# A last block whose attention heads go through the array in pairs, in a fixed order among the projections

## The chip, the cores and the metric

The kernel runs on one core of a Trainium2 chip. The metric is the device time of one execution in microseconds (us). A core has five engines that run their own queues in order and wait for each other by semaphores: TensorE (PE in the profile; its weight loads are listed apart as PEld) multiplies matrices, VectorE (DVE) and ScalarE (ACT) work elementwise and empty PSUM, the memory that TensorE writes, GpSimd (POOL) works elementwise out of SBUF, and SyncE (SP) starts DMA transfers.

## The reference

256 tokens of 1024 channels in float32 go through three blocks: a first layer of two parallel mixers, a layer of latent attention, each followed by a squared-ReLU feed-forward part, and then the last block, which the change touches:

```
def chunk_relpos_attention(h, w_qkv, w_o, rel_bias):   # 16 heads of 64
    q, k, v = split_heads(h, w_qkv)
    ...
    for c in range(n_chunks):                          # chunks of 64 queries
        sc = einsum('bhqd,bhkd->bhqk', q_blk, k[:, :, k0:k1]) / sqrt(64)
        p = softmax(sc + bias, axis=-1)                # bias by relative position, per head
        outs.append(einsum('bhqk,bhkd->bhqd', p, v[:, :, k0:k1]))
    return merge_heads(o) @ w_o

x = x + rms_norm(chunk_relpos_attention(rms_norm(x, g), w_qkv, w_o, rel_bias), g_post)
x = x + rms_norm((silu(h @ w_gate) * (h @ w_up)) @ w_down, g_post_ffn)
```

With 256 tokens a query chunk sees all keys up to its own chunk. Every product is float32.

## The kernel before

Activations lie in SBUF with 128 channels on the partitions: `xh` and `xl` hold x as a high and a low part, and each weight block is split in the same way as it streams in, `whi` on ScalarE (line 149) and `wlo` on VectorE or GpSimd (line 152, class `Stream`). A product is then three fast matmuls, high by high, high by low, low by high. `mgemm` (lines 419 to 451) computes 256 tokens by 512 outputs, with the tokens as weights of the array and 512 weight columns streaming: eight blocks of 128 input channels (k), two token tiles, three matmuls each, into two PSUM banks. `tgemm_tok` (lines 453 to 491) does this for 1024 outputs in four banks; its first four k go in 8 steps (k by token tile) of two column halves, its last four k tile by tile. PSUM is used through two rings of four banks, `mmt()` and `auxt()`.

The stage in question is the value projection (two calls of `mgemm`, 512 outputs each), the attention of 16 heads, and the output projection (`tgemm_tok`). A head needs four steps: `sc` (scores of 256 queries in two tiles: the first against 128 keys, the second against 256; heads alternate between the upper and lower 64 partitions of `qT` and `kT`; VectorE adds the bias and takes the maximum, ScalarE takes exponentials and sums), `nrm` (VectorE scales by the reciprocal sum), `tr` (three 128x128 transposes on TensorE, copied out by VectorE for even and ScalarE for odd heads) and `pv` (probabilities times values, 64 output rows; after an odd head ScalarE and VectorE split the pair into `yh` and `yl`). These products are plain float32 matmuls, not split ones, and the profile shows each as two records. `attend(i)` issues `tr(i-3)`, `pv(i-4)`, `nrm(i-1)`, `sc(i)`. Three such calls are handed to `later`, a list of callbacks that run after so many microseconds of issued matmuls, in the second value projection; the rest follow after it, and four are issued within the output projection. In what order an engine's queue holds this work is decided by a scheduler, by a simulated time line; only the output projection's TensorE queue is kept in the order of the code (`manual_schedule`, before `tgemm_tok`).

Of the kernel before, what the change touches and what calls it, by code (L numbers as in the profile page):

```python
# [10 lines left out]
F32 = mybir.dt.float32  # L11
F32R = mybir.dt.float32r
# [6 lines left out]
P = 128  # L19
# [174 lines left out]
def block_kernel(ctx, tc, a, out):  # L194
# [18 lines left out]
    def mmt():  # L213
        return mm.tile([P, 512], F32, tag="mm", name="mm")

    def auxt():
        return aux.tile([P, 512], F32, tag="aux", name="aux")
# [198 lines left out]
        if b:  # L416
            S.done()

    def mgemm(h, l, nk, evac, per=4, psum=None, apart=False):


        pss = [(psum or mmt)() for _ in range(2)]
        n = nk // per

        def part(tt, k, w):
            wh, wl = w
            s = slice(k % per * 512, (k % per + 1) * 512)
            ts = slice(tt * P, (tt + 1) * P)
            pe.matmul(pss[tt], h[k][:, ts], wh[:, s], start=k == 0, stop=False)  # L429
            pe.matmul(pss[tt], h[k][:, ts], wl[:, s], start=False, stop=False)  # L430
            pe.matmul(pss[tt], l[k][:, ts], wh[:, s], start=False, stop=k == nk - 1)  # L431
            later.tick(0.65)

        if apart:
            ws = [S.get() for _ in range(n)]
            S.done(held=n)
            for tt in range(2):
                for k in range(nk):
                    part(tt, k, ws[k // per])
                evac(tt, pss[tt])  # L440
        else:
            for c in range(n):
                w = S.get()
                for k in range(c * per, (c + 1) * per):
                    for tt in range(2):
                        part(tt, k, w)
                if c < n - 1:
                    S.done()
            for tt in range(2):
                evac(tt, pss[tt])  # L450
        S.done()

    def tgemm_tok(h, l, nk, evac, psum, pre={}):
# [12 lines left out]

        step = 0
        for k in range(nk - 4):
            if k % 2 == 0:
                w = S.get()  # L470
            for tt in range(2):
                if step in pre:
                    pre[step]()
# [418 lines left out]
    with tc.tile_pool(name="mla", bufs=1) as ap:  # L892
# [229 lines left out]
    ss = b2.tile([P, 2, 2], F32, name="ss")  # L1122
    ss2 = b2.tile([P, 2, 2], F32, name="ss2")
    r1 = b2.tile([P, 2], F32, name="r1")

    def row(i):

# [12 lines left out]
    with tc.tile_pool(name="cra", bufs=1) as ap, tc.tile_pool(name="crt", bufs=2) as mp:  # L1140
# [15 lines left out]
        qT = ap.tile([P, 8, T], F32, name="qT")  # L1156
        kT = ap.tile([P, 8, T], F32, name="kT")
        v = ap.tile([P, 2, D], F32, tag="v", name="v")
        yh = ap.tile([P, KB, T], F32R, name="yh")
        yl = ap.tile([P, KB, T], F32R, name="yl")  # L1160
        R = ap.tile([P, 2], F32, name="R")

        def qk_chain():
# [26 lines left out]
        def qk_out(m, ps):  # L1190
            g = ps.shape[1]
            for i in range(g):
                j = m + i
                dst, rb = (qT[:, j], rbc[1]) if j < 8 else (kT[:, j - 8], rbc[0])
                state["qk"] = dve.tensor_tensor(dst, ps[:, i], rb, op=ALU.mult)

        later(3.5, qk_chain)
# [6 lines left out]
        st_p, st_t = {}, {}  # L1204

        QS = (slice(0, P), slice(P, 3 * P))

        def sc(h):
            ps = mmt()
            rr = slice(64 * (h % 2), 64 * (h % 2) + 64)  # L1210
            j = h // 2
            pe.matmul(ps[:, QS[0]], qT[rr, j, 0:P], kT[rr, j, 0:P], start=True, stop=True)
            pe.matmul(ps[:, QS[1]], qT[rr, j, P:T], kT[rr, j], start=True, stop=True)
            mx = mp.tile([P, 2], F32, tag="mx", name="mx", bufs=3)
            nm = mp.tile([P, 2], F32, tag="nm", name="nm", bufs=3)
            sm = mp.tile([P, 2], F32, tag="sm", name="sm", bufs=4)
            sb = mp.tile([P, 3 * P], F32, tag="sb", name="sb", bufs=2)
            pr = mp.tile([P, 3 * P], F32, tag="pr", name="pr", bufs=4)
            dve.tensor_tensor_reduce(sb[:, QS[0]], ps[:, QS[0]], B[:, h, P:T], op0=ALU.add, op1=ALU.max,
                                     scale=1.0, scalar=-3.0e38, accum_out=mx[:, 0:1])  # L1220
            dve.tensor_tensor_reduce(sb[:, QS[1]], ps[:, QS[1]], B[:, h], op0=ALU.add, op1=ALU.max,
                                     scale=1.0, scalar=-3.0e38, accum_out=mx[:, 1:2])
            dve.tensor_scalar(nm, mx, -1.0, None, op0=ALU.mult)
            for qt in range(2):
                act.activation(pr[:, QS[qt]], sb[:, QS[qt]], AF.Exp, bias=nm[:, qt:qt + 1],
                               accum_out=sm[:, qt:qt + 1])
            st_p[h] = (pr, sm)

        def nrm(h):
            pr, sm = st_p[h]  # L1230
            dve.reciprocal(sm, sm)
            for qt in range(2):
                dve.tensor_scalar(pr[:, QS[qt]], pr[:, QS[qt]], sm[:, qt:qt + 1], None, op0=ALU.mult)

        def tr(h):
            pr, sm = st_p.pop(h)
            ps = auxt()
            for i in range(3):
                pe.transpose(ps[:, i * P:(i + 1) * P], pr[:, i * P:(i + 1) * P], ident)
            pT = mp.tile([P, 3 * P], F32, tag="pT", name="pT", bufs=2)  # L1240
            (act.activation(pT, ps[:, 0:3 * P], AF.Copy) if h % 2 else dve.tensor_copy(pT, ps[:, 0:3 * P]))
            st_t[h] = pT

        def pv(h):
            pT = st_t.pop(h)
            if h % 2 == 0:
                state["o"] = auxt()
            o = state["o"]
            rr = slice(64 * (h % 2), 64 * (h % 2) + 64)
            hc = slice(h * 64, (h + 1) * 64)  # L1250
            pe.matmul(o[rr, 0:T], v[:, 0, hc], pT[:, 0:T], start=True, stop=False)  # L1251
            pe.matmul(o[rr, P:T], v[:, 1, hc], pT[:, T:3 * P], start=False, stop=True)
            if h % 2:
                j = h // 2
                S.behind = act.activation(yh[:, j], o[:, 0:T], AF.Copy)
                dve.tensor_tensor(yl[:, j], o[:, 0:T], yh[:, j].bitcast(F32), op=ALU.subtract)

        def attend(i):
            if 0 <= i - 3 < NH:
                tr(i - 3)  # L1260
            if 0 <= i - 4 < NH:
                pv(i - 4)
            if 0 <= i - 1 < NH:
                nrm(i - 1)
            if i < NH:
                sc(i)
# [4 lines left out]
        mgemm(XH, XL, KB, v_evac(0))  # L1271
        for i in range(3):
            later(3.8 + 2.0 * i, lambda i=i: attend(i))
        mgemm(XH, XL, KB, v_evac(1), psum=auxt)
        later.flush()
        for i in range(3, NH):
            attend(i)

        mix_row = row(1)

# [17 lines left out]
        def x_feat(tt, b):  # L1298
# [16 lines left out]
        mctx = tc.manual_schedule(engines={mybir.EngineType.PE})  # L1315
        mctx.__enter__()
        tgemm_tok(per_k(yh), per_k(yl), KB, wo_evac, mmt,
                  pre={2: lambda: attend(16),4: lambda: attend(17),6: lambda: attend(18),7: lambda: attend(19)})


    with tc.tile_pool(name="swi", bufs=1) as ap, tc.tile_pool(name="swt", bufs=2) as mp:
# [181 lines left out]
```

## Time and profile before

| | us |
|---|---|
| median of 3 runs | 928.31 (924.77, 928.31, 928.44) |
| profiled execution | 924.32 |
| its span, first to last instruction | 922.6 |
| TensorE busy | 898.3 |
| VectorE, ScalarE, GpSimd busy | 588.8, 482.8, 253.8 |
| mean granted TensorE clock | 0.994 of full speed |

Times within the span are us from its start. The profile's records of matmuls overlap, since they are pipelined; how fast TensorE goes is read from the distance between starts, not from the length of a record.

### The profile page before, as it was taken

The page shows a single profiled execution, that of the slowest core. Times are in us where ns is not written, and L with a number is a line of the kernel's source. Part 1 is how long each engine was busy: PE and PEld are TensorE (multiplying, and loading weights), DVE is VectorE, ACT ScalarE, POOL GpSimd, SP SyncE. Part 2 cuts the span into 40 slices and gives each one's busy share as a digit, 9 for nine tenths or more (in the row PEclk, how much of TensorE's full clock was granted, in tenths as well). Part 3 has the DMA queues.
Part 4 walks back from the last instruction along what each step waited for, and adds up shares of the span by engine and source line. Part 5 has one row for each costly group of instructions (what it writes and reads, how often), then busy time and mean ns, then how long its engine had stood idle before and what let it go on. Part 6 is the DMA issues. An engine that isn't in the chain of part 4 may idle for free.

```text
span 922.6 us, 16429 instructions
## 1 busy us (share of the span) xinstructions
PE 898.3 (97%) x6680; PEld 829.2 (90%) x6680; DVE 588.8 (64%) x975; ACT 482.8 (52%) x848; POOL 253.8 (28%) x253
## 2 busy tenths in 40 slices
PE   8899999999999988999999999999999999999997
PEld 6789999999999977679999999999866789999885
DVE  7697789555555389727855555548574776666442
ACT  6685458554444366656655444434464665544331
POOL 5877633332011284058233111100221100000000
PEclk9999999999999999999999999999999999999999
DMA  8543454555554244024655555568420465555521
GB/s 286 205 170 124 162 188 164 202 189 183 189 189 168 85 161 183 1 92 183 229 183 183 184 187 186 184 188 307 185 92 1 164 234 191 208 186 185 186 86 45
DMA packets 26107, 154.90 MB, mean 168 GB/s; under 512 B 2752, under 2 KB 5744, under 8 KB 8752
## 3 DMA queue, kind: packets, MB, share of 16 engines
q1 hardware_dynamic: 22704, 148.70, 45.5%
q10 hardware_dynamic: 3040, 4.36, 1.8%
q8 instruction: 52, 0.85, 0.4%
q0 software_dynamic: 288, 0.79, 0.3%
q14 instruction: 23, 0.19, 0.1%
HBM read 152.25 MB, written 1.07 MB: 166 GB/s over the span
## 4 chain that ended last, share of the span: by engine, by line
PE 58%; DVE 2%; issue 0%; ACT 0%; DVEq 0%; POOLq 0%; ACTq 0%
PE mm L368 12%; PE mm L369 12%; PE mm L370 12%; PE aux L464 2%; PE aux L462 2%; PE aux L463 2%; PE aux L1059 2%; PE mm L1025 1%; PE mm L431 1%; PE mm L430 1%; PE mm L429 1%; PE aux L1251 1%; PE aux L1047 1%; PE mm L462 1%; PE mm L464 1%; PE mm L463 1%
## 5 line engine op out<-in xcount | busy, mean ns | idle before, releaser
L149 ACT ACTIVATE whi<-raw 128x1024 fp32r<-128x1024 f32 (+3 forms) x318 | 284.3, 949 | 247.8 <-PE mm L369 152.4
L152 DVE TENSOR_TENSOR wlo<-raw,whi 128x1024 fp32r<-128x1024 f32 (+2 forms) x254 | 306.4, 1243 | 126.2 <-ACT whi L149 124.6
L368 PE MATMUL mm<-xh,whi 128*128 128x256 f32 x1072 | 301.8, 282 | 0.8 <-DVE head L491 0.8
L370 PE MATMUL mm<-xh,wlo 128*128 128x256 f32 x1072 | 299.6, 280 | 0.0
L369 PE MATMUL mm<-xl,whi 128*128 128x256 f32 x1072 | 299.5, 280 | 0.0
L370 PEld LDWEIGHTS mm<-xh,wlo 128*128 128x128 f32 x1072 | 204.4, 191 | 0.0
L368 PEld LDWEIGHTS mm<-xh,whi 128*128 128x128 f32 x1072 | 202.5, 189 | 1.7 <-DVE head L491 1.0
L369 PEld LDWEIGHTS mm<-xl,whi 128*128 128x128 f32 x1072 | 202.5, 189 | 0.2
L370 PE MATMUL mm<-hh,wlo 128*128 128x256 f32 x512 | 143.9, 281 | 0.0
L369 PE MATMUL mm<-hl,whi 128*128 128x256 f32 x512 | 143.9, 281 | 0.0
L368 PE MATMUL mm<-hh,whi 128*128 128x256 f32 x512 | 143.9, 281 | 0.0
L152 POOL TENSOR_TENSOR wlo<-raw,whi 128x512 fp32r<-128x512 f32 (+2 forms) x64 | 84.5, 1348 | 109.5 <-ACT whi L149 109.5
L370 PEld LDWEIGHTS mm<-hh,wlo 128*128 128x128 f32 x512 | 98.3, 192 | 0.0
L368 PEld LDWEIGHTS mm<-hh,whi 128*128 128x128 f32 x512 | 96.1, 188 | 0.0
L369 PEld LDWEIGHTS mm<-hl,whi 128*128 128x128 f32 x512 | 96.1, 188 | 0.0
L516 POOL TENSOR_TENSOR fu<-ft 128x512 f32<-128x512 f32 (+1 forms) x36 | 54.6, 1519 | 118.9 <-ACT ft L514 111.1
L313 POOL TENSOR_TENSOR s_acc<-s_acc,sq 128x256 f32<-128x256 f32 x37 | 43.8, 1189 | 155.1 <-ACT sq L312 144.5
L1117 POOL TENSOR_TENSOR r<-v,nhalf 128x1 f32<-128x1 f32 x4 | 2.2, 546 | 190.4 <-DVE v L1116 190.4
L517 DVE TENSOR_TENSOR hl<-fu,hh 128x512 fp32r<-128x512 f32 (+1 forms) x36 | 24.0, 674 | 23.4 <-POOL fu L516 23.4
L463 PE MATMUL aux<-wlo,hh 128*128 128x512 f32 x88 | 34.8, 396 | 0.0
L464 PE MATMUL aux<-whi,hl 128*128 128x512 f32 x88 | 34.8, 395 | 0.0
L462 PE MATMUL aux<-whi,hh 128*128 128x512 f32 x88 | 34.8, 395 | 0.0
(382 smaller groups left out, 1381.0 us busy)
## 6 DMA issues: line engine op xcount, KB each, us to landing
raw<-in_w_dram SPq DMA_DIRECT2D x64, 1024.0 KB, 4.9
raw<-in_w_gu_dram SPq DMA_DIRECT2D x22, 1024.0 KB, 4.8
raw<-in_w_qk_dram SPq DMA_DIRECT2D x12, 1024.0 KB, 5.8
raw<-in_w_down_dram SPq DMA_DIRECT2D x11, 1024.0 KB, 4.8
raw<-in_w_ab_out_dram SPq DMA_DIRECT2D x4, 1024.0 KB, 4.8
raw<-in_w_c_out_dram SPq DMA_DIRECT2D x4, 1024.0 KB, 4.7
raw<-in_w_v_dram SPq DMA_DIRECT2D x4, 1024.0 KB, 5.9
raw<-in_w_o_dram SPq DMA_DIRECT2D x4, 1024.0 KB, 4.8
```

The source lines that it names most:

```text
L149: self.nc.scalar.activation(hi[:, s], r[:, s], AF.Copy)
L152: eng.tensor_tensor(lo[:, s], r[:, s], hi[:, s].bitcast(F32), op=ALU.subtract)
L313: state["sum"] = (dve if k == last else pool).tensor_tensor(acc, acc, sq, op=ALU.add)
L368: pe.matmul(ps, wh, h, start=start, stop=False)
L369: pe.matmul(ps, wh, l, start=False, stop=False)
L370: pe.matmul(ps, wl, h, start=False, stop=stop)
L462: pe.matmul(ps, h[k][:, ts], wh[:, ns], start=k == 0, stop=False)
L463: pe.matmul(ps, h[k][:, ts], wl[:, ns], start=False, stop=False)
L464: pe.matmul(ps, l[k][:, ts], wh[:, ns], start=False, stop=k == nk - 1)
L516: pool.tensor_tensor(u[:, 0:g], t[:, 0:g], t[:, 0:g], op=ALU.mult)
L517: dve.tensor_tensor(hl[:, m:m + g], u[:, 0:g], hh[:, m:m + g].bitcast(F32), op=ALU.subtract)
L1059: pe.matmul(o[rr, 0:T], v[:, kt, h * 64:(h + 1) * 64], pT[:, kt], start=kt == 0, stop=kt == 1)
```

## The change

Heads go in pairs. `sc(j)` computes heads 2j and 2j+1 with their matmuls alternating between the upper and the lower 64 rows of the array, into two banks; `pv(j)` computes both heads' values, alternating between the left and the right 64 columns of the array, into the two halves of one bank. Maximum, negation, sum and reciprocal are held for a pair in tiles of four columns. The biased scores go straight into `pr`, which the exponential then overwrites. The scaling of the second head of each pair moves from VectorE to GpSimd. `qT`, `kT`, `yh` and `yl` become eight tiles each, and `yh[j]` takes the room of `qT[j]`, `yl[j]` that of `kT[j]`. All of the attention is issued from a `hook` inside the projections: step s counts the k of the two value projections (0 to 15) and the steps of the output projection (16 to 23), and pair j has its scores ahead of step 2j, its transposes ahead of 2j+7 and its value product ahead of 2j+9. TensorE's queue is now kept in the order of the code from the first value projection on. A tile of 8 columns (32 bytes) that nothing uses is put in front of the last block's tiles.

```diff
-    def mgemm(h, l, nk, evac, per=4, psum=None, apart=False):
+    def mgemm(h, l, nk, evac, per=4, apart=False, hook=None):
...
+        pss = [mmt() for _ in range(2)]
...
                 for k in range(c * per, (c + 1) * per):
+                    if hook:
+                        hook(k)
...
+    b2.tile([P, 8], F32, name="pad_b2")
...
+        def sc(j):
+
+            pss = [auxt(), auxt()]
+            for qt in range(2):
+                for i, rr in enumerate(HALF):
+                    pe.matmul(pss[i][:, QS[qt]], qT[j][rr, qt * P:(qt + 1) * P], kT[j][rr, KS[qt]],
+                              start=True, stop=True)
...
+                    (pool if i else dve).tensor_scalar(prs[i][:, QS[qt]], prs[i][:, QS[qt]], sm[:, c:c + 1], None,
+                                                       op0=ALU.mult)
...
+            for kt in range(2):
+                for i, rr in enumerate(HALF):
+                    pe.matmul(o[rr, kt * P:T], v[:, kt, (2 * j + i) * 64:(2 * j + i + 1) * 64],
+                              pTs[i][:, T * kt:T + P * kt], start=kt == 0, stop=kt == 1)
...
+            for j in range(NH // 2):
+                if s == 2 * j + 9:
+                    pv(j)
+            for j in range(NH // 2):
+                if s == 2 * j + 7:
+                    tr(j)
+            for j in range(NH // 2):
+                if s == 2 * j + 2:
+                    nrm(j)
+                if s == 2 * j:
+                    sc(j)
...
+        mctx = tc.manual_schedule(engines={mybir.EngineType.PE})
+        mctx.__enter__()
+        mgemm(XH, XL, KB, v_evac(0), hook=attend)
+        mgemm(XH, XL, KB, v_evac(1), hook=lambda k: attend(8 + k))
...
+        tgemm_tok(yh, yl, KB, wo_evac, mmt, hook=lambda s: attend(16 + s))
```

On TensorE, behind the value projection before (L1213 and L1212 are scores, L1251 and L1252 values, L1239 transposes), heads stand one after another without projection work between them:

```order
L1251 MATMUL aux<-pT,v 64x256
L1252 MATMUL aux<-pT,v 64x128
L1239 MATMUL aux<-ident,pr 128x128 x3
L1212 MATMUL mm<-kT,qT 128x128
L1213 MATMUL mm<-kT,qT 128x256
L1251 MATMUL aux<-pT,v 64x256
L1252 MATMUL aux<-pT,v 64x128
L1212 MATMUL mm<-kT,qT 128x128
L1213 MATMUL mm<-kT,qT 128x256
L1212 MATMUL mm<-kT,qT 128x128
L1213 MATMUL mm<-kT,qT 128x256
```

Of these rows none is left where it stands: the change takes all attention work out of this stretch and puts it among the projections.

On TensorE after the change, in the second value projection (L430 to L432 are the projection's, L1219 scores, L1269 values, L1257 transposes):

```order
L1219 MATMUL aux<-kT,qT 128x128 x2
L1219 MATMUL aux<-kT,qT 128x256 x2
L430 MATMUL mm<-whi,xh 128x512
L431 MATMUL mm<-wlo,xh 128x512
L432 MATMUL mm<-whi,xl 128x512
L430 MATMUL mm<-whi,xh 128x512
L431 MATMUL mm<-wlo,xh 128x512
L432 MATMUL mm<-whi,xl 128x512
L1269 MATMUL aux<-pT,v 64x256 x2
L1269 MATMUL aux<-pT,v 64x128 x2
L1257 MATMUL aux<-ident,pr 128x128 x6
```

Scores, values and transposes of a pair each have six projection matmuls between them now, and both heads of a pair stand together.

On GpSimd, before, the twelve low parts of the output projection's weights follow each other behind the last mask of the bias (L1188):

```order
L324 TENSOR_TENSOR R<-v_6990,nhalf 128x2
L1188 MEMSET B 64x4x64 x4
L152 TENSOR_TENSOR wlo<-raw,whi 128x512 x12
L1117 TENSOR_TENSOR r_6909<-v_8153,nhalf 128x1
L1117 TENSOR_TENSOR r_6909<-v_8218,nhalf 128x1
```

The run of twelve is what the change splits.

On GpSimd after the change, from the scaling of the sixth pair on (L1248 is the scaling):

```order
L1248 TENSOR_SCALAR pr<-pr,sm 128x128
L1248 TENSOR_SCALAR pr<-pr,sm 128x256
L152 TENSOR_TENSOR wlo<-raw,whi 128x512
L1248 TENSOR_SCALAR pr<-pr,sm 128x128
L1248 TENSOR_SCALAR pr<-pr,sm 128x256
L152 TENSOR_TENSOR wlo<-raw,whi 128x512 x3
L1248 TENSOR_SCALAR pr<-pr,sm 128x128
L1248 TENSOR_SCALAR pr<-pr,sm 128x256
L152 TENSOR_TENSOR wlo<-raw,whi 128x512 x8
```

Six pairs' scalings now come ahead of the first of these twelve subtractions, and two more among them.

On ScalarE after the change, around the evacuation of the first value projection (L1238 are exponentials, L1259 a copy of transposed probabilities, L1292 the evacuation, L1274 `yh`):

```order
L1238 ACTIVATE pr,sm<-pr,nm 128x128
L1238 ACTIVATE pr,sm<-pr,nm 128x256
L149 ACTIVATE whi<-raw 128x1024
L1259 ACTIVATE pT<-aux 128x384
L1292 ACTIVATE v<-mm,R 128x512 x2
L1274 ACTIVATE yh<-aux 128x256
L149 ACTIVATE whi<-raw 128x1024
```

Before, the two evacuations of the first half stood among weight splits, ahead of all exponentials; now the exponentials of four pairs, a weight split and a copy come ahead of them.

## Rows read from the trace of the kernel before

**Rows 1.** The page's first part: engine, busy us, share, instructions.
```profile
PE 898.3 (97%) x6680; PEld 829.2 (90%) x6680; DVE 588.8 (64%) x975; ACT 482.8 (52%) x848; POOL 253.8 (28%) x253
```

**Rows 2.** Stage table: window, length, busy us by engine, granted clock, DMA share, GB/s.
```profile
652.38:730.49 78.11, 78.11 (x379) 55.87 (x378) 46.56 (x167) 42.47 (x118) 16.03 (x14) 1.00 0.30 108
```

**Rows 3.** TensorE in time order: start us, us, line, operation; value projection.
```profile
652.38 0.39 PE L429 MATMUL mm<-whi,xh 128*128 128x512 f32 x1
...
667.25 0.40 PE L431 MATMUL aux<-whi,xl 128*128 128x512 f32 x1
667.58 0.48 PE L1212 MATMUL mm<-kT,qT 64*128 64x128 f32 x2
...
668.76 0.39 PE L430 MATMUL aux<-wlo,xh 128*128 128x512 f32 x1
```

**Rows 4.** TensorE in time order, attention between the projections.
```profile
683.48 0.50 PE L1212 MATMUL mm<-kT,qT 64*128 64x128 f32 x4
683.81 0.61 PE L1213 MATMUL mm<-kT,qT 64*128 64x256 f32 x4
684.35 0.55 PE L1239 MATMUL aux<-ident,pr 128*128 128x128 f32 x3
...
689.06 0.48 PE L1212 MATMUL mm<-kT,qT 64*128 64x128 f32 x2
...
689.91 0.65 PE L1251 MATMUL aux<-pT,v 128*64 128x256 f32 x2
690.39 0.38 PE L1252 MATMUL aux<-pT,v 128*64 128x128 f32 x2
690.71 0.55 PE L1239 MATMUL aux<-ident,pr 128*128 128x128 f32 x3
```

**Rows 5.** TensorE in time order, a product in four column strips, second layer.
```profile
326.12 1.07 PE L363 MATMUL aux<-head,ws 128*32 128x256 f32 x16
327.12 0.39 PE L369 MATMUL mm<-cl,whi 128*128 128x256 f32 x1
```

**Rows 6.** TensorE in order, output projection; three transposes lie between the first two.
```profile
700.87 0.39 PE L464 MATMUL mm<-whi,yl 128*128 128x512 f32 x1
...
701.67 0.40 PE L463 MATMUL mm<-wlo,yh 128*128 128x512 f32 x1
...
715.81 0.40 PE L464 MATMUL mm<-whi,yl 128*128 128x512 f32 x1
...
717.26 0.39 PE L463 MATMUL mm<-wlo,yh 128*128 128x512 f32 x1
...
727.29 0.39 PE L464 MATMUL mm<-whi,yl 128*128 128x512 f32 x1
...
728.20 0.39 PE L463 MATMUL mm<-wlo,yh 128*128 128x512 f32 x1
```

**Rows 7.** VectorE's scalings and GpSimd's subtractions in time order; a GpSimd scaling group.
```profile
671.16 0.55 DVE L1233 TENSOR_SCALAR pr<-pr,sm 128x128 f32<-128x128 f32 x2
...
674.15 2.61 DVE L1233 TENSOR_SCALAR pr<-pr,sm 128x128 f32<-128x128 f32 x2
...
671.52 5.09 POOL L152 TENSOR_TENSOR wlo<-raw,whi 128x512 fp32r<-128x512 f32 x4 [1.64 <-ACT whi L149]
...
L812 POOL TENSOR_SCALAR sg<-sg 128x512 f32<-128x512 f32 x2 | 2.2, 1091 | 2.6 <-ACT sg L811 2.6
```

**Rows 8.** ScalarE in time order, value projection.
```profile
658.07 2.01 ACT L149 ACTIVATE whi<-raw 128x1024 fp32r<-128x1024 f32 x2 [3.55 <-PE mm L431]
662.88 1.38 ACT L1269 ACTIVATE v<-mm,R 128x512 f32<-128x512 f32 x2 [2.80 <-PE mm L431]
...
669.94 0.40 ACT L1225 ACTIVATE pr<-sb,nm 128x128 f32<-128x128 f32 x1 [3.61 <-DVE nm L1223]
...
670.83 2.18 ACT L149 ACTIVATE whi<-raw 128x512 fp32r<-128x512 f32 x4
```

**Rows 9.** A group of the page's fifth part: count, busy us, mean ns.
```profile
L463 PE MATMUL aux<-wlo,hh 128*128 128x512 f32 x88 | 34.8, 396 | 0.0
```

More of the change, by code (lines that the diff above doesn't have):

```diff
@@ L417, in tgemm @@
             S.done()
-    def mgemm(h, l, nk, evac, per=4, psum=None, apart=False):
-        pss = [(psum or mmt)() for _ in range(2)]
+    def mgemm(h, l, nk, evac, per=4, apart=False, hook=None):
+        pss = [mmt() for _ in range(2)]
         n = nk // per
@@ L451, in mgemm, with tgemm_tok @@
         S.done()
-    def tgemm_tok(h, l, nk, evac, psum, pre={}):
+    def tgemm_tok(h, l, nk, evac, psum, hook=None):
         pss = [[psum() for _ in range(2)] for _ in range(2)]
@@ L471, in tgemm_tok @@
             for tt in range(2):
-                if step in pre:
-                    pre[step]()
+                if hook:
+                    hook(step)
                 step += 1
@@ L1154, in block_kernel @@
                 tensor=src.tensor, offset=src.offset + 127 - 32 * q - 31, ap=[[1, 32], [LX, NH], [1, T]]))
-        qT = ap.tile([P, 8, T], F32, name="qT")
-        kT = ap.tile([P, 8, T], F32, name="kT")
+        qT = [ap.tile([P, T], F32, tag="q", name="qT", bufs=8) for _ in range(8)]
+        kT = [ap.tile([P, T], F32, tag="k", name="kT", bufs=8) for _ in range(8)]
         v = ap.tile([P, 2, D], F32, tag="v", name="v")
-        yh = ap.tile([P, KB, T], F32R, name="yh")
-        yl = ap.tile([P, KB, T], F32R, name="yl")
+        yh, yl = [None] * KB, [None] * KB
         R = ap.tile([P, 2], F32, name="R")
@@ L1193, in qk_out @@
                 j = m + i
-                dst, rb = (qT[:, j], rbc[1]) if j < 8 else (kT[:, j - 8], rbc[0])
+                dst, rb = (qT[j], rbc[1]) if j < 8 else (kT[j - 8], rbc[0])
                 state["qk"] = dve.tensor_tensor(dst, ps[:, i], rb, op=ALU.mult)
@@ L1206, in block_kernel @@
         QS = (slice(0, P), slice(P, 3 * P))
[L1208 to L1222, printed above, removed]
-            dve.tensor_scalar(nm, mx, -1.0, None, op0=ALU.mult)
[L1224 to L1227, printed above, removed]
@@ L1229, in nrm @@
-        def nrm(h):
-            pr, sm = st_p[h]
-            dve.reciprocal(sm, sm)
[L1232 to L1266, printed above, removed]
+        KS = (slice(0, P), slice(0, T))
+        HALF = (slice(0, 64), slice(64, P))
+        def sc(j):
[4 more added lines that the diff above has]
+                              start=True, stop=True)
+            later.tick(0.65)
+            mx = mp.tile([P, 4], F32, tag="mx", name="mx", bufs=3)
+            nm = mp.tile([P, 4], F32, tag="nm", name="nm", bufs=3)
+            sm = mp.tile([P, 4], F32, tag="sm", name="sm", bufs=5)
+            prs = []
+            for i in range(2):
+                pr = mp.tile([P, 3 * P], F32, tag="pr", name="pr", bufs=10)
+                prs.append(pr)
+                for qt in range(2):
+                    c = 2 * i + qt
+                    dve.tensor_tensor_reduce(pr[:, QS[qt]], pss[i][:, QS[qt]], B[:, 2 * j + i, P * (1 - qt):T],
+                                             op0=ALU.add, op1=ALU.max, scale=1.0, scalar=-3.0e38,
+                                             accum_out=mx[:, c:c + 1])
+            dve.tensor_scalar(nm, mx, -1.0, None, op0=ALU.mult)
+            for i in range(2):
+                for qt in range(2):
+                    c = 2 * i + qt
+                    S.behind = act.activation(prs[i][:, QS[qt]], prs[i][:, QS[qt]], AF.Exp, bias=nm[:, c:c + 1],
+                                              accum_out=sm[:, c:c + 1])
+            st_p[j] = (prs, sm)
@@ new lines, in nrm, with tr @@
+        def nrm(j):
+            prs, sm = st_p[j]
+            dve.reciprocal(sm, sm)
+            for i in range(2):
+                for qt in range(2):
+                    c = 2 * i + qt
+                    (pool if i else dve).tensor_scalar(prs[i][:, QS[qt]], prs[i][:, QS[qt]], sm[:, c:c + 1], None,
+                                                       op0=ALU.mult)
+        def tr(j):
+            prs, sm = st_p.pop(j)
+            st_t[j] = []
+            for i in range(2):
+                ps = auxt()
+                for n in range(3):
+                    pe.transpose(ps[:, n * P:(n + 1) * P], prs[i][:, n * P:(n + 1) * P], ident)
+                pT = mp.tile([P, 3 * P], F32, tag="pT", name="pT", bufs=4)
+                (act.activation(pT, ps[:, 0:3 * P], AF.Copy) if i else dve.tensor_copy(pT, ps[:, 0:3 * P]))
+                st_t[j].append(pT)
+            later.tick(0.65)
@@ new lines, in pv @@
+        def pv(j):
+            pTs = st_t.pop(j)
+            o = auxt()
+            for kt in range(2):
+                for i, rr in enumerate(HALF):
+                    pe.matmul(o[rr, kt * P:T], v[:, kt, (2 * j + i) * 64:(2 * j + i + 1) * 64],
+                              pTs[i][:, T * kt:T + P * kt], start=kt == 0, stop=kt == 1)
+            later.tick(0.65)
+            yh[j] = ap.tile([P, T], F32R, tag="q", name="yh", bufs=8)
+            yl[j] = ap.tile([P, T], F32R, tag="k", name="yl", bufs=8)
+            S.behind = act.activation(yh[j], o[:, 0:T], AF.Copy)
+            dve.tensor_tensor(yl[j], o[:, 0:T], yh[j].bitcast(F32), op=ALU.subtract)
@@ L1268, in v_evac, with attend @@
+        def attend(s):
+            for j in range(NH // 2):
[9 more added lines that the diff above has]
+                    sc(j)
         def v_evac(n):
             return lambda tt, ps: act.activation(v[:, tt, n * 512:(n + 1) * 512], ps, AF.Copy, scale=R[:, tt:tt + 1])
-        mgemm(XH, XL, KB, v_evac(0))
@@ L1272, in block_kernel @@
[L1272 to L1277, printed above, removed]
+        mctx = tc.manual_schedule(engines={mybir.EngineType.PE})
+        mctx.__enter__()
+        mgemm(XH, XL, KB, v_evac(0), hook=attend)
+        mgemm(XH, XL, KB, v_evac(1), hook=lambda k: attend(8 + k))
         mix_row = row(1)
@@ L1313, in x_feat @@
                     square(xt[:, tt, n * 512:(n + 1) * 512], ss2[:, tt, n:n + 1], RD)
[L1315 to L1318, printed above, removed]
+        tgemm_tok(yh, yl, KB, wo_evac, mmt, hook=lambda s: attend(16 + s))
     with tc.tile_pool(name="swi", bufs=1) as ap, tc.tile_pool(name="swt", bufs=2) as mp:
```

## Prediction

> **What bounds the kernel now.** I read the busy shares first, then the table of stages, then the instructions of the stage that the diff touches in order of time. TensorE is busy for 898.3 of 922.6 us [rows 1], so whatever does not shorten TensorE's own queue cannot shorten the span. The change lies in one stage: from the first matmul of the value projection at 652.38 us [rows 3] to the end of the output projection at 730.49 us. There TensorE is busy for all of 78.11 us, at the full granted clock of 1.00, while VectorE has 46.56, ScalarE 42.47 and GpSimd 16.03 us of work [rows 2]. Before the change no other engine is waited for in this stage; TensorE is simply full. So a saving counts in full if it is time that TensorE spends, and a new wait on TensorE costs in full as well.
>
> What is in those 78.11 us? The value projection has 96 matmuls of 512 columns. From 652.38 to 667.25 there are 65 starts, so one takes 0.2288 us [rows 3], and 96 take 21.97 us. The output projection also has 96; from 717.26 to 727.29 there are 43 starts, 0.2333 us each [rows 6], so 22.39 us. The transposes of x after it come in two groups; from 727.29 to 728.20 is 0.91 us with two ordinary matmuls in it, so 0.44 us a group and 0.9 us for both [rows 6]. What is left, 78.11 - 21.97 - 22.39 - 0.9 = 32.85 us, is the attention of 16 heads: 2.05 us a head, or 4.11 us a pair.
>
> **The change part by part.** (a) *Scores, two heads in the two row halves.* One head between full matmuls takes 667.25 to 668.76, 1.51 us, of which two matmuls are 0.46: 1.05 us for the head [rows 3]. One head in a run of attention work takes 689.06 to 689.91, 0.85 us [rows 4]; the other 0.20 us is entering and leaving the half-height form. Whether halves run side by side can be read off the kernel before, by luck: at 683.48 the scheduler put two heads of unlike parity next to each other, four records of each line where a head has two, and both are through at 684.35, in 0.87 us [rows 4]. So a pair costs what one head costs. In the new order each pair stands between full matmuls: 0.87 + 0.20 = 1.07 us, 8 pairs, 8.6 us.
>
> (b) *Values, two heads in the two column halves.* One head takes 689.91 to 690.71, 0.80 us [rows 4], and 0.98 us between full matmuls (715.81 to 717.26, less 2 x 0.233) [rows 6]. No two heads of this line stand together before. The nearest row is the gate product with four heads of 32 columns each: 16 records, which are 8 matmuls, from 326.12 to 327.12, 1.00 us [rows 5]; one after another at the 0.48 us that a 256-column matmul takes at 689.91 [rows 4] they would be 3.84. So column strips run side by side too. Bounds for a pair: 0.98 us if they do fully, 0.98 + 0.80 = 1.78 if not. I take 0.98, since the row has four strips in the time of one: 8 pairs, 7.8 us.
>
> (c) *Transposes.* These use the whole array and do not shrink. Three take 700.87 to 701.67, 0.80 - 0.47 = 0.33 us between full matmuls [rows 6]; three more behind them I take at 0.25, since the entry of about 0.1, half of the 0.20 in (a), is not paid twice, so 0.58 us a pair and 4.6 us in all.
>
> New attention on TensorE: 8.6 + 7.8 + 4.6 = 21.0 us instead of 32.85: 11.8 us less.
>
> (d) *What the fixed order can cost.* Before, the scheduler chose at each point what was ready. Now TensorE's order is written out, and a matmul that waits holds the whole queue behind it. I walked the new order with durations of before. A step of the value projection is 6 matmuls, 1.37 us. The scores of a pair have their softmax done well ahead: seven steps and three score pairs lie between scores and transposes, over 12 us, while four reductions on VectorE (about 1.1), four exponentials on ScalarE (669.94 to 670.83 is one head, 0.89 [rows 8]; 1.8 a pair) and the scaling need some 5. Two places are tight. The first value product needs v from PSUM: the two evacuations take 1.38 us on ScalarE [rows 8] and can start only when the last matmul of the first half ends; the new order gives them 1.07 + 1.37 = 2.44 us, but ScalarE has a weight split of 1.0 us (2.01 for two [rows 8]) and a copy of transposed probabilities queued ahead of them. That leaves about 0.7 us of wait. The fifth value product repeats this for the other half, 0.6. And the scores of a pair take the PSUM bank that the value product two steps earlier has to give back, by way of ScalarE and VectorE: three times, 0.1 to 0.3 us by the walk. Together 1.7 us. Bounds: nothing, and 2.3 us at each of the first two places if a pair's exponentials also stand ahead (1.8 + 1.0 + 1.4 + 0.5 = 4.7 against 2.44), so 4.6 us.
>
> (e) *Scaling of every second head moved to GpSimd.* GpSimd scales 512 columns in 1.091 us [rows 7], so 384 columns take about 0.8 us (an estimate from that row); with 512-column subtractions at 1.27 us each (5.09 for four [rows 7]) the upper bound is 2.5 us a pair. The twelve weight subtractions of the output projection now stand behind the first six pairs there. The last one would be done about 51 us into the stage and is needed after 54, so they stay hidden behind the steps of the output projection; were they later than that, TensorE would pay each microsecond. The weight loads that these subtractions release start later for the first and earlier for the last; DMA is busy for 0.30 of the stage [rows 2]. I cost this at nothing. The danger is the other direction. At 674.15 two scalings on VectorE took 2.61 us instead of the 0.55 of 671.16, while GpSimd ran its subtractions from 671.52 on [rows 7]. VectorE is slowed by 2.06 us when it meets GpSimd. Now both scale halves of one pair at the same time, eight times. Bounds: 0 and 8 x 2.06 = 16.5 us, if none of it had slack. I take 0, because seven steps of slack lie behind it.
>
> The Trainium skill, page SBUF — State Buffer, section Who interferes with whom, says that VectorE in a two-port mode and GpSimd exclude each other for a whole instruction, and that the one that issued first blocks the other. The trace agrees: 2.61 us against 0.55. By that rule the two scalings of each pair will always collide, which raises the chance of the slower rival below; the sum would still be the same as long as the slack holds.
>
> (f) *Smaller edits.* Reductions write into the probability tile instead of a scratch tile, and negation and reciprocal handle four columns at once, half as many instructions on engines that have room: nothing. The extra 32 bytes shift the tiles behind them. Matmuls with yh take 0.2333 and with xh 0.2288 us [rows 3, 6], and the down projection's 264 have the slow form's length of 396 ns [rows 9]; were the shift to bring the fast pace to all 360, it would give 360 x 0.0045 = 1.6 us, and the reverse is as thinkable. I take 0.
>
> **Sum.** 11.8 - 1.7 = 10.1 us. The profiled execution of before took 924.32 us (span 922.6), so 914.2 us on its footing. That execution is 4.0 us below the median of the runs shown, 928.31, and 0.4 below the fastest. I put the forecast midway between the sum on the profile (914.2) and the sum on the median (918.2): 916.
>
> **Rivals.**
> *A, the evacuation takes over.* The fixed order waits on ScalarE at its upper bound, 4.6 us at two places, and at the bank hand-backs up to 0.5 us three times: 6.1 us. For it: ScalarE's queue has weight splits among the exponentials. Against it: 42.47 us of work in 68. Gain 11.8 - 6.1 = 5.7, time 918.6 on the profile's footing and 922.6 on the median's.
> The Trainium skill, page TensorEngine Tiling (Array Packing), section Performance Considerations, says that tiling speeds up TensorE but not the emptying of PSUM, which may become the bound. By that rule this rival is the natural result; the trace of before, with VectorE busy 0.6 of the stage, neither shows nor excludes it.
> *B, slower: VectorE and GpSimd block each other at the scaling.* Place: the scaling of each pair, price 2.06 us a pair and 16.5 us for eight, time 914.2 + 16.5 = 930.7 on the profile. It decides against the change from 10.1/8 = 1.3 us a pair on TensorE's path. For it: the row at 674.15. Against it: the slack of over 7 us behind each scaling, and VectorE's load of 46.56 less the 8 heads moved.
> *C, halves do not run side by side here.* Then scores cost 8 x 0.85 and values 8 x 0.80 more, 13.2 us, and the waits of (d) vanish: 924.32 - 11.8 + 13.2 = 925.7, no change. If only the columns fail, 6.4 us are lost: gain 3.7, time 920.6 on the profile. For it: only the score form was seen in pairs. Against it: [rows 4, 5].
>
> **How the numbers follow.** Forecast 0.68, A 0.16, C 0.10 (its two forms alike), B 0.06. A difference under 0.5% (4.6 us on 928.31, so 923.7 to 933.0) is about what cannot be told from none. The forecast counts as faster, A too but for 0.02 of its 0.16, C as the same but for 0.03; of B I give 0.04 to slower and 0.02 to the same. Faster 0.85, same 0.11, slower 0.04. Range: 910 (the full 11.8 with the 1.6 of (f), on the profile's footing, 910.9) to 923 (A at its worst on the median's footing, 922.6).
>
> **What would show it.** Four records of each score line through in about 0.87 us, and a value pair in about 0.8; the stage about 68 us instead of 78.11; TensorE's idle time inside it 1 to 3 us, ahead of the first and fifth value products, with ScalarE's v as the releaser. A pair of value products at 1.6 us shows C, idle time ahead of the transposes with VectorE or GpSimd as the releaser shows B, and idle time ahead of the scores or over 4 us in sum shows A. Time lost or won outside the stage would show that the shift of addresses matters, and make the sum wrong.

## The result, and the profile after the change

The changed kernel takes 914.45 us (median of 4 runs, 913.52 to 918.1) against 927.05 for the kernel before on the same chip: ratio 0.9874, interval 0.9838 to 0.991, so 1.3% faster. The profiled execution is the slowest of the four, 918.1 us with a span of 916.4; that of before took 924.32 with 922.6.

The first two rows below are the stage table of after, in the columns of [rows 2]: the stage of the change, and all that follows it. The third is the same for what follows in the kernel before, which runs from 730.49 to its end.

```profile
657.48:724.26 66.78, 66.78 (x378) 48.61 (x377) 41.33 (x135) 42.07 (x119) 29.71 (x30) 1.00 0.34 127
724.26:916.40 192.14, 184.66 (x1243) 167.22 (x1241) 109.84 (x154) 87.69 (x130) 2.35 (x4) 0.99 0.44 162
```

```profile
730.49:922.60 192.11, 184.66 (x1243) 167.18 (x1241) 109.88 (x154) 87.70 (x130) 2.33 (x4) 1.00 0.45 162
```

The stage went from 78.11 us [rows 2] to 66.78, 11.33 us less, and TensorE is still busy for every bit of it. What follows is unchanged, 192.1 us. VectorE's work fell from 46.56 to 41.33 us, and GpSimd's rose from 16.03 to 29.71.

The two spans differ by only 6.2 us, because the stage begins at 657.48 here and at 652.38 before. That is not the change: the same program, profiled once more below, began the stage at 652.82. One place where this profile lost time is the stretch from 360 to 370 us, ahead of anything that the change touches: its granted clock there was 0.66 of full speed, in the repeat and in the kernel before 1.00. So every run is read by the length of its stage first, and by its ratio second.

TensorE of after in time order (start us, us, line, operation), a pair of scores among full matmuls; it answers to [rows 3]:

```profile
660.97 0.40 PE L432 MATMUL mm<-whi,xl 128*128 128x512 f32 x1
661.29 0.93 PE L1219 MATMUL aux<-kT,qT 64*128 64x128 f32 x8
...
662.48 0.39 PE L431 MATMUL mm<-wlo,xh 128*128 128x512 f32 x1
...
665.10 0.93 PE L1219 MATMUL aux<-kT,qT 64*128 64x128 f32 x8
```

From 660.97 to 662.48 is 1.51 us: to the digit what one head took before, 667.25 to 668.76 [rows 3], now with eight records for two heads. From pair to pair, 661.29 to 665.10, lie 3.81 us; less 12 matmuls at 0.2288 that leaves 1.06 us for the pair.

The same for a pair's values and the next pair's transposes, to set beside [rows 4]:

```profile
675.53 0.40 PE L432 MATMUL mm<-whi,xl 128*128 128x512 f32 x1
675.85 0.87 PE L1269 MATMUL aux<-pT,v 128*64 128x256 f32 x8
676.65 0.88 PE L1257 MATMUL aux<-ident,pr 128*128 128x128 f32 x6
677.28 0.48 PE L430 MATMUL mm<-whi,xh 128*128 128x512 f32 x1
677.60 0.40 PE L431 MATMUL mm<-wlo,xh 128*128 128x512 f32 x1
```

The values of two heads take 675.85 to 676.65, 0.80 us, what one head took at 689.91 [rows 4]. Values and transposes together cost 677.60 - 675.53 - 0.46 = 1.61 us.

GpSimd's (first) and VectorE's scalings of after, beside [rows 7]; the last row of GpSimd is the last two of its weight subtractions in this stage:

```profile
663.09 1.68 POOL L1248 TENSOR_SCALAR pr<-pr,sm 128x128 f32<-128x128 f32 x2 [3.15 <-DVE sm L1244]
...
689.37 1.55 POOL L1248 TENSOR_SCALAR pr<-pr,sm 128x128 f32<-128x128 f32 x2 [2.40 <-DVE sm L1244]
...
707.34 2.53 POOL L152 TENSOR_TENSOR wlo<-raw,whi 128x512 fp32r<-128x512 f32 x2 [1.88 <-ACT whi L149]
```

```profile
663.43 0.55 DVE L1248 TENSOR_SCALAR pr<-pr,sm 128x128 f32<-128x128 f32 x2
...
...
694.42 0.73 DVE L1248 TENSOR_SCALAR pr<-pr,sm 128x128 f32<-128x128 f32 x2
```

GpSimd needs 1.53 to 1.68 us for its head, not 0.8, and VectorE's scaling beside it stretches from 0.55 to 0.73 at most; the 2.61 us of [rows 7] do not come back. GpSimd's last subtractions end at 709.87, and TensorE never waits for them.

### The profile page after: what moved, and what is told of

It is laid out like the page before. It is cut to its first block, busy times and chain, and to the rows that moved or that the text cites. A ratio compares the mean times of both kernels' runs of the same rounds, so it can differ in the third digit from the quotient of the medians.

```text
span 916.4 us, 16411 instructions
## 1 busy us (share of the span) xinstructions
PE 889.9 (97%) x6680; PEld 824.1 (90%) x6680; DVE 583.3 (64%) x943; ACT 481.3 (53%) x848; POOL 268.0 (29%) x269
## 3 DMA queue, kind: packets, MB, share of 16 engines
HBM read 152.25 MB, written 1.07 MB: 167 GB/s over the span
## 4 chain that ended last, share of the span: by engine, by line
PE 58%; DVE 1%; issue 0%; ACT 0%; DVEq 0%; POOLq 0%; ACTq 0%
PE mm L368 12%; PE mm L369 12%; PE mm L370 12%; PE aux L466 2%; PE aux L465 2%; PE aux L467 2%; PE mm L1028 2%; PE aux L1062 2%; PE mm L430 2%; PE mm L432 2%; PE mm L431 2%; PE aux L1050 1%; PE mm L465 1%; PE mm L467 1%; PE mm L466 1%; PE aux L1219 1%
## 5 line engine op out<-in xcount | busy, mean ns | idle before, releaser
L430 PE MATMUL mm<-whi,xh 128*128 128x512 f32 x96 | 39.1, 424 | 1.9 <-ACT whi L149 1.9
L431 PE MATMUL mm<-wlo,xh 128*128 128x512 f32 x96 | 38.1, 400 | 2.2 <-DVE wlo L152 2.2
L432 PE MATMUL mm<-whi,xl 128*128 128x512 f32 x96 | 37.9, 398 | 0.6 <-DVE xl L1329 0.6
```

## The experiments

Two theories stood against each other. Mine: the gain is that two half-size matmuls run side by side. The rival: the gain is the even spread in a fixed order. Each run is a change to the kernel after. The stage is the length of the last block's stage (before: 78.11); the ratio is to the kernel before, run beside it. The runs were made on three chips, so medians of different rows are better compared by their ratios.

| run | stage us | median us | ratio, interval |
|---|---|---|---|
| after again | 66.80 | 913.75 | 0.9853 [0.9833, 0.9872] |
| one head, then the other | 67.87 | 914.60 | 0.9868 [0.9842, 0.9893] |
| scores and values apart | 81.80 | 929.73 | 1.0028 [1.0012, 1.0044] |
| values apart | 73.87 | 921.80 | 0.9944 [0.992, 0.9969] |
| scaling on VectorE | 69.62 | 918.43 | 0.9886 [0.9846, 0.9926] |
| no pad | 66.72 | 915.85 | 0.9860 [0.9824, 0.9897] |
| scheduler free in the value projection | 71.22 | 919.95 | 0.9912 [0.9878, 0.9946] |
| pairs in the second layer too | 66.80 | 910.88 | 0.9812 [0.9779, 0.9846] |
| the same, loop in fixed order | 66.93 | 912.96 | 0.9824 [0.9792, 0.9855] |
| the same, output projection too | 66.91 | 914.17 | 0.9832 [0.9799, 0.9864] |
| the same, one step more of lag | 66.79 | 906.66 | 0.9758 [0.9727, 0.9788] |

**After again.** No edit.

> The changed kernel once more, as the measure for the runs beside it. Both theories: the last block's stretch (first value-projection or score matmul to first gate matmul) again 66.8 us +-0.3 against 78.1 before, the time 0.984 to 0.991 of before's.

As expected: two profiles of one program give the stage to 0.02 us, and the four runs below that leave the last block as it is lie between 66.79 and 66.93, so differences of a few tenths can be told apart.

**Side by side, or evenly spread?** Two runs keep the fixed order and every projection matmul's place, and part the heads of a pair. In the first, the second head's scores stand one step of six matmuls later, and in 7 of 8 pairs the next pair's six transposes lie between the two heads' values:

```
-                if s == 2 * j:
-                    sc(j)
+                if s in (2 * j, 2 * j + 1):
+                    sc(j, s - 2 * j)
```
```
+            for i, rr in enumerate(HALF):
+                if i:
+                    between()
+                for kt in range(2):
```

> The heads of a pair are kept apart in the fixed order: the second head's score product stands one step of the value projection later, and its value product behind the next pair's six transposes (7 of 8 pairs). Everything else, the order of the projections included, stays. Theory (the gain is that two heads run side by side): scores 8 x 1.05 = +8.4 us, values 7 x (0.80 to 0.98) = +5.6 to 6.9 us, the stretch 80.8 to 82.1 us, the time about 929. Rival (the gain is the even spread in a fixed order, which leaves no gaps): stretch at most 70 us, time at most 918.

The second run has only the last edit:

> Only the value products of a pair are kept apart (the next pair's six transposes between them, 7 of 8 pairs), the score products stay in pairs. Theory (side by side): +5.6 to 6.9 us, the stretch 72.4 to 73.7 us, the time about 920.5. Rival (even spread): stretch within 1 us of the changed kernel's 66.8. Together with the run in which both are apart this gives the scores' share as the difference, 8.4 us expected.

TensorE with both apart: a head's scores, and two heads' values with the transposes between them.

```profile
655.49 0.92 PE L1226 MATMUL aux<-kT,qT 64*128 64x128 f32 x4
656.34 0.50 PE L430 MATMUL mm<-whi,xh 128*128 128x512 f32 x1
...
678.05 0.86 PE L1276 MATMUL aux<-pT,v 128*64 128x256 f32 x4
678.85 0.87 PE L1262 MATMUL aux<-ident,pr 128*128 128x128 f32 x6
679.65 0.86 PE L1276 MATMUL aux<-pT,v 128*64 128x256 f32 x4
680.45 0.92 PE L1226 MATMUL aux<-kT,qT 64*128 64x128 f32 x4
```

Four records of scores now take 0.85 us, as eight did; each head's values take 0.80, as two heads' did. The stage is 7.07 us longer with the values apart, 1.01 a pair, a little above the range given; the scores add 81.80 - 73.87 = 7.93 us, of which 0.43 is one wait for v. With both apart the fixed order alone is 3.7 us slower than the kernel before. The rival falls.

**Must the two halves take turns?** In the kernel after, the four matmuls of a pair alternate between the heads. Here one head's two come first:

```
-            for kt in range(2):
-                for i, rr in enumerate(HALF):
+            for i, rr in enumerate(HALF):
+                for kt in range(2):
```

(and likewise in the scores).

> Within a pair the two matmuls of one head stand together and then the two of the other, instead of taking turns. Theory (the array starts a matmul on free rows or columns as soon as it is at the head of the queue, and one head's two matmuls are short enough to be overlapped by the next head's): the stretch stays 66.8 us +-1. Rival (only a matmul whose direct neighbour sits on the other half lies beside it): of a pair's four matmuls only the middle two overlap, half the gain goes: about +0.4 us per pair of scores and +0.4 per pair of values, +6.4 us, stretch 73; if nothing overlaps, +13 us, stretch 80.

The stage is 67.87 us, so the overlap does not depend on the alternation. Of the 1.07 us, 1.03 sit at two places. TensorE of this run, a pair of scores, then its first and its fifth value pair:

```profile
668.38 0.93 PE L1219 MATMUL aux<-kT,qT 64*128 64x128 f32 x8
669.25 0.50 PE L430 MATMUL mm<-whi,xh 128*128 128x512 f32 x1
...
670.83 1.23 PE L1269 MATMUL aux<-pT,v 128*64 128x256 f32 x8
671.99 0.87 PE L1257 MATMUL aux<-ident,pr 128*128 128x128 f32 x6
...
691.59 0.40 PE L467 MATMUL mm<-whi,yl 128*128 128x512 f32 x1
692.06 1.45 PE L1269 MATMUL aux<-pT,v 128*64 128x256 f32 x8
693.44 0.88 PE L1257 MATMUL aux<-ident,pr 128*128 128x128 f32 x6
```

And the fifth value pair of the kernel after:

```profile
696.24 0.40 PE L467 MATMUL mm<-whi,yl 128*128 128x512 f32 x1
...
697.42 0.88 PE L1257 MATMUL aux<-ident,pr 128*128 128x128 f32 x6
```

The scores still take 0.87 us for two heads. The first value pair takes 1.16 us instead of 0.80, and the fifth, from the matmul ahead of it, 1.85 instead of 1.18: 0.36 + 0.67 = 1.03 us. ScalarE's evacuation of v in the kernel after:

```profile
674.94 1.24 ACT L1292 ACTIVATE v<-mm,R 128x512 f32<-128x512 f32 x2
```

It fills v in two pieces, one for each half of the tokens. In the kernel after, the value pair starts at 675.85, when only the first piece is done; both heads use that piece first, and the second piece, done at 676.18, is wanted only by their second matmuls. With one head first, its second matmul wants the second piece at once. So the alternation is worth about 1 us, for another reason than the array's.

**Is GpSimd's scaling a cost or a help?**

```
-                    (pool if i else dve).tensor_scalar(prs[i][:, QS[qt]], prs[i][:, QS[qt]], sm[:, c:c + 1], None,
+                    dve.tensor_scalar(prs[i][:, QS[qt]], prs[i][:, QS[qt]], sm[:, c:c + 1], None,
```

> The second head's scaling goes from GpSimd (1.53 to 1.68 us a pair) back to VectorE (some 0.55 us a pair more there). Theory (both engines have slack in this stretch, TensorE is never idle): stretch 66.8 +-0.3, time within 0.3% of the changed kernel's. Rival (GpSimd's help is part of the gain): VectorE's 8 x 0.55 = 4.4 us come up as waits, the stretch 68 to 71 us. Other rival (GpSimd's slow scaling holds the values back): the stretch shorter by 0.5 us or more.

My theory failed: 2.8 us longer. TensorE, VectorE and GpSimd of this run at the largest of its waits:

```profile
693.96 0.87 PE L1269 MATMUL aux<-pT,v 128*64 128x256 f32 x8 [1.23 <-DVE yl L1275]
```

```profile
667.45 1.01 DVE L1248 TENSOR_SCALAR pr<-pr,sm 128x128 f32<-128x128 f32 x4
...
690.50 3.08 DVE L1248 TENSOR_SCALAR pr<-pr,sm 128x128 f32<-128x128 f32 x4
693.49 0.41 DVE L1275 TENSOR_TENSOR yl<-aux,yh 128x256 fp32r<-128x256 f32 x1
```

```profile
690.85 3.86 POOL L152 TENSOR_TENSOR wlo<-raw,whi 128x512 fp32r<-128x512 f32 x3 [4.16 <-ACT whi L149]
```

Four scalings that take 1.01 us alone take 3.08 while GpSimd subtracts. The subtraction yl of an earlier value pair stands behind them, the PSUM bank comes back late, and the next value pair waits 1.23 us; 1.2 us of waits for v are the rest that the trace names, 2.4 of the 2.8 us in all. Seven steps of slack lie behind the scalings themselves, but not behind what is queued after them. With GpSimd scaling, it cannot subtract at that moment: the changed split keeps the collision of [rows 7] out of this stage.

The Trainium skill, SBUF — State Buffer, Who interferes with whom, says that the engine that issues first holds the shared ports for the whole instruction. By that rule GpSimd's scalings would block VectorE's as its subtractions do. The trace agrees for the subtractions, 3.08 against 1.01 us, but not for GpSimd's scalings, beside which VectorE's two take 0.55 to 0.73: in three pairs GpSimd had started first (663.09, 666.26 and 680.63), and VectorE's two took 0.55, 0.62 and 0.55 us.

**The pad.** The line that allocates the extra 32 bytes is left out.

> The changed kernel without the 32-byte pad that moves the buffers behind it. Theory (addresses cost nothing here): stretch 66.8 +-0.3, and from the first gate matmul to the end 192.1 us as in both kernels so far. Rival (addresses matter): one of these two differs by about 1.6 us or more.

```profile
651.81:718.53 66.72, 66.72 (x377) 48.58 (x377) 41.49 (x134) 42.09 (x119) 29.77 (x30) 1.00 0.35 127
718.53:910.70 192.17, 184.66 (x1243) 167.18 (x1241) 109.91 (x154) 87.67 (x130) 2.36 (x4) 0.99 0.45 162
```

The stage and what follows it are the same to 0.1 us: this shift of addresses costs nothing here.

**Is the fixed order needed?** The two lines that fix TensorE's order move from ahead of the value projection to ahead of the output projection.

> The pairs stay, but the fixed order of TensorE's work holds only from the output projection on; in the value projection the scheduler places the score pairs itself. Theory (pairing is the gain, the order only has to keep TensorE fed): stretch 66 to 68 us. Rival (without the fixed order TensorE waits for the softmax or the evacuations): 70 us or more, with named waits in the trace.

My theory failed again: 71.22 us, TensorE busy for 69.36 of them. TensorE in this run, three of the four single heads of scores and the two waits:

```profile
684.46 0.92 PE L1219 MATMUL aux<-kT,qT 64*128 64x128 f32 x4
...
689.92 0.92 PE L1219 MATMUL aux<-kT,qT 64*128 64x128 f32 x4
691.20 0.92 PE L1219 MATMUL aux<-kT,qT 64*128 64x128 f32 x4
...
697.09 0.87 PE L1269 MATMUL aux<-pT,v 128*64 128x256 f32 x8 [0.62 <-DVE sm L1244]
699.21 0.86 PE L1269 MATMUL aux<-pT,v 128*64 128x256 f32 x6 [1.25 <-ACT pT L1259]
```

The scheduler parts two of the eight score pairs (four records each, 0.85 us each) and cuts a value pair in two; that is most of the 2.56 us of added busy time. It also leaves scores to the end, so that their softmax is waited for: 0.62 + 1.25 = 1.87 us. The fixed order's first use is that it keeps pairs together.

**A second place for pairs.** The attention of the second layer computes the values of sixteen heads one by one, each in one column half. Here a head's product is held back until its neighbour's can stand beside it:

```
+            pTs = [st_t.pop(h - 1), st_t.pop(h)]
+            o = auxt()
+            for kt in range(2):
+                for i in range(2):
+                    pe.matmul(o[64 * i:64 * i + 64, 0:T], v[:, kt, (h - 1 + i) * 64:(h + i) * 64], pTs[i][:, kt],
+                              start=kt == 0, stop=kt == 1)
```

> In addition the value products of the second layer's attention run in pairs on the two column halves. There one head's value product takes 1.01 us now (sixteen of them). Theory (two column halves run side by side wherever they are neighbours): 8 x about 0.95 = 7.6 us less in that layer's attention, the time about 907. Rival (that stage is bound by the softmax or the evacuations, not by TensorE): TensorE's busy time falls by 7 to 8 us there and its idle time rises by as much, the time within 0.3% of the changed kernel's 914.5.

From the first score of that layer to the first matmul of the last block passed 292.62 us in the kernel after (its second profile, 360.20 to 652.82) and 289.02 here (362.31 to 651.33): 3.6 us less, half of what I expected. The granted clock from 360 to 370 us was 1.00 there and 0.83 here; the two runs with the heads apart, which leave this layer as it is and also had 0.83, took 293.5 us, so at a like clock it is 4.5 us less. TensorE, first of the kernel after (second profile), then of this run:

```profile
371.50 1.08 PE L1062 MATMUL aux<-pT,v 128*64 128x256 f32 x4
372.51 0.66 PE L1050 MATMUL aux<-ident,pr 128*128 128x128 f32 x4
```

```profile
372.15 0.65 PE L1062 MATMUL aux<-pT,v 128*64 128x256 f32 x2
372.72 0.55 PE L1050 MATMUL aux<-ident,pr 128*128 128x128 f32 x3
...
374.07 1.08 PE L1062 MATMUL aux<-pT,v 128*64 128x256 f32 x6
375.07 0.66 PE L1050 MATMUL aux<-ident,pr 128*128 128x128 f32 x4
```

One head took 1.01 us. The pair takes 0.57 for its first matmul, which the scheduler set apart, and 1.00 for the other three: 8 x (2.02 - 1.57) = 3.6 us by these rows. Two more runs fix TensorE's order in the loop over the heads, and in the output projection behind it too:

```
+        mctx = tc.manual_schedule(engines={mybir.EngineType.PE})
+        mctx.__enter__()
         for i in range(3, NH):
             attend(i)
+        mctx.__exit__(None, None, None)
```

> As the run with pairs in two layers, and TensorE's order is fixed in the second layer's loop over the heads, so that the four matmuls of a value pair stand together there (six of eight pairs). With the scheduler's free order each pair was cut in two pieces that took 0.58 + 1.01 = 1.59 us from start to start, against 2 x 1.01 for two single heads. Theory (the cut is what cost the expected gain): 6 x (1.59 - 1.01) = 3.5 us less than that run, the time about 907. Rival (ScalarE and VectorE, each with about 1.8 us of work per head there, and the softmax's latency take over as soon as TensorE's 1.95 us per head wait for a fixed turn): waits of TensorE on pr or pT in the loop, no gain or a loss, 911 or more.

> The same with the fixed order kept through the output projection behind the loop, so that all eight value pairs stand together. Theory: 8 x 0.58 = 4.6 us less than the run with free order, about 906. Rival: as in the run with the fixed loop alone, waits on pr, pT or yl eat it, 911 or more.

Neither gains over the run before: 912.96 and 914.17 us, and the stretch of the first is 290.21 us against 289.02, both at a granted clock of 0.83 from 360 to 370 us. Their pairs stand together, but TensorE now waits for the softmax, 2.6 us in six waits ahead of transposes. The first of the two:

```profile
367.88 0.63 PE L1050 MATMUL aux<-ident,pr 128*128 128x128 f32 x4 [1.45 <-DVE pr L1043]
...
383.60 0.81 PE L1050 MATMUL aux<-ident,pr 128*128 128x128 f32 x4 [0.20 <-DVE pr L1043]
384.34 1.08 PE L1062 MATMUL aux<-pT,v 128*64 128x256 f32 x8
...
388.73 1.08 PE L1062 MATMUL aux<-pT,v 128*64 128x256 f32 x8
```

A pair comes every 4.39 us, 384.34 to 388.73, where two single heads took 2 x 2.46 (371.50 above to the next at 373.96), but a wait stands ahead of many of them and the first costs 1.45 us. The written order has each head's transposes three steps behind its scores; the scheduler had put the scores of five heads ahead of the first transpose. (The profile of the second of the two also had a granted clock of 0.58 and 0.74 from 360 to 370 and 370 to 380 us, so its 294.46 us for the whole stretch is not compared.) The next run starts from the second and gives every head one step more:

```
-            if 0 <= i - 3 < NH:
-                tr(i - 3)
+            if 0 <= i - 4 < NH:
+                tr(i - 4)
```

(and values at five steps, with the last steps placed accordingly.)

> The same as the last, with each head's transposes and values one step later behind its scores (four and five steps instead of three and four). If waits on the softmax's latency eat the gain of the fixed order, they go here and the time falls to about 906; if the pairs' gain already shows in full with three steps, nothing changes beyond 0.3%; if ScalarE or VectorE are the bound by their work, nothing changes either and their busy share in the loop is near 100%.

TensorE of this run, and its stretch from 370 to 380 us in the columns of [rows 2]:

```profile
367.80 1.08 PE L1062 MATMUL aux<-pT,v 128*64 128x256 f32 x8
368.81 1.13 PE L1028 MATMUL mm<-kT,qT 96*128 96x256 f32 x4
...
371.62 1.08 PE L1062 MATMUL aux<-pT,v 128*64 128x256 f32 x8
```

```profile
370.00:380.00 10.00, 10.00 (x68) 7.40 (x66) 9.58 (x33) 8.75 (x27) 0.00 (x0) 1.00 0.00 0
```

A pair comes every 3.82 us, and TensorE no longer waits between pairs (1.5 us in two waits at the start of the loop are left). The stretch is 286.05 us, 6.6 less than in the kernel after (second profile), both at a granted clock of 1.00 from 360 to 370 us, and the median 906.66 us: ratio 0.9758, interval 0.9727 to 0.9788, better than both kernels. VectorE is busy for 9.58 of the 10 us there, so little more is to be had from TensorE's side of that loop.

## Why the prediction was right, point by point

It said 916 us from a saving of 10.1 us in the stage. The stage gave 11.33, and the median was 914.45. That the two times lie so close is in part luck: the saving was put 1.2 us too low, and the base, midway between the profiled execution and the median (926.3), 0.7 below the 927.05 of the comparison; the two errors work against each other.

- **The frame held.** TensorE is the only bound of the stage before and after, so its own time counts in full; what follows the stage did not move. The medians are 12.6 and, in the second comparison, 13.8 us below before, 1.3 and 2.5 us more than the stage accounts for, a difference that lies within the first comparison's interval and just outside the second's; no row shows where it would be.
- **(a) Scores**: 1.07 us a pair foreseen, 1.06 found. The two heads that stood side by side by luck before were the right row to read. Parting them again costs 7.5 us without the one wait for v.
- **(b), (c) Values and transposes**: 0.98 + 0.58 = 1.56 foreseen, 1.61 found; 0.4 us in all. Column halves behave as row halves, and the row with four column strips was a fair guide.
- **(d) Waits of the fixed order**: 1.7 us foreseen, none found, and the sign named for them, idle time ahead of the first and fifth value products, did not come. This term was mis-sized. The walk made the first and the fifth value product wait for both pieces of v; only their second matmuls need the second piece. The run with one head first, where they do wait for both, has 1.03 us more at exactly these two places, against the 1.3 of the walk. The three bank hand-backs cost nothing.
- **(e) GpSimd's scaling** takes about 1.55 us a pair, not 0.8, inside the bound, and is hidden as said. But the step priced the move only as a possible harm. Taken back, it costs 2.8 us: the relief of VectorE at the moment when GpSimd would be subtracting is part of what makes the stage free of waits. The reason given, seven steps of slack behind each scaling, does not cover what stands behind it in VectorE's queue.
- **(f) The pad** costs nothing, as said. The merged negations and reciprocals were not taken back by themselves, so what they are worth is not shown.
- **The rivals.** A, the evacuation takes over: not in the kernel after, but the run with the scaling on VectorE shows its mechanism, 2.4 us of waits on v and on a bank. B, VectorE and GpSimd block each other: not in the kernel after, where VectorE's scalings take 0.73 us at most and not 2.61. C, halves do not run side by side: both runs that part them show its price, and the kernel after does not pay it.

## What to carry to other kernels

Look in the trace for half-height or half-width products that stand next to each other by chance: they give the price of a pair before it is built. A pair pays in full only while its matmuls are neighbours, so keep the scheduler from parting them, and then give the fixed order as much lag as the scheduler had taken. Order the products inside a pair so that what is evacuated first is used first.

## What the runs showed of the hardware

- Two heads' matmuls in the two row halves or column halves take the time of one (0.86 against 0.85 us, 0.80 against 0.80), and it does not matter whether they alternate or stand two and two (scores 0.86 and 0.87 us, values 0.80 and 0.81 where none of them waits).
- VectorE's four scalings of a pair took 1.01 us alone and 3.08 beside GpSimd's TENSOR_TENSOR, but beside GpSimd's TENSOR_SCALAR two took 0.55 to 0.73. (GpSimd's own times are rough.)
- The full matmuls of the output projection kept about 0.233 us against 0.229 in the value projection, with the pad or without; why is still open.
